# The gate of a differential attention kernel is multiplied in by GpSimd when a group leaves PSUM

## The chip, the cores and the metric

One core of one Trainium2 chip runs the kernel. The metric is the device time of one execution in microseconds, the median of several runs. Nothing below the 0.2% that separates runs of the same kernel (2296.99 to 2302.23 us here) is read as a change.

## What is computed

The reference is one layer of a transformer with differential attention: an adaptive RMS norm of 2048 latent tokens and 256 context tokens, a projection to q, k, v and a gate z, two softmaxes for each head, a norm over each head's 128 output channels, the gate, an output projection, the residual and a last RMS norm. What matters here is the end of it:

```python
def diff_attend(q, k, v, lam):
    s = jnp.einsum('bqhzd,bkhzd->bhzqk', q, k).astype(jnp.float32)
    p = jax.nn.softmax(s, axis=-1)
    a = p[:, :, 0] - lam * p[:, :, 1]
    return jnp.einsum('bhqk,bkhe->bqhe', a.astype(v.dtype), v)
...
    def finish(o, z):
        of = o.astype(jnp.float32)
        of = of * lax.rsqrt(jnp.mean(of * of, axis=-1, keepdims=True) + SUBLN_EPS)
        of = of * subln_gain.astype(jnp.float32) * (1.0 - lambda_init)
        return (of.reshape(B, L, D).astype(z.dtype) * jax.nn.silu(z)) @ w_out
```

There are 8 heads, 2048 queries and 2304 keys. The value that goes into the last matmul is thus, for each head, channel and query, the product of three numbers: the attention output `o`, a factor `f` of the query (the norm) and the gate (silu of z times the gain of the channel).

## The kernel before

The kernel works in three stages, each with a list of steps that a planner (`Plan`) puts in order from the costs and due times written beside each step. Each compute engine executes its instructions in that order. The DMA transfers are all issued from SyncE's queue (SP), in one order too, so a transfer that waits holds up those behind it.

`project` (0 to about 830 us) makes q, k, v and the gate and stores them to DRAM; the gate goes to `gate_d[h]`, one tile of 128 channels by 2048 queries for each head.

`attend` (about 830 to 2110 us) goes through 64 groups, 8 for each head, of 256 queries each (two units of 128, `u`, and two softmaxes, `z`). In a group TensorE computes the scores (`qk`, L688) into PSUM in chunks of 768 keys, VectorE copies each chunk to SBUF and keeps its minimum (`keep`, L699), ScalarE takes the exponentials (`expo`, L717), VectorE a reciprocal (`ratio`, L721), and then GpSimd weighs the second softmax (`weigh`, L729) and adds it to the first (`join`, L733). The joined probabilities are turned by TensorE (`turn`, L740), split into a high and a low part by ScalarE (`high`, L749) and VectorE (`low`, L754, which reads the low part's source from PSUM and the high part from SBUF), and multiplied with v (`pv`, L763). The turn of a group is planned some ten chunks after its scores, so TensorE has scores of the next groups to do meanwhile. At the end of a group ScalarE copies the output from PSUM to the tile `ot` (`evac`, L771), which is stored to `o_d[h]`; GpSimd clamps a copy of it (`clamp`, L776), ScalarE squares it (L779, L783), GpSimd takes the low part (`sq_low`, L787), and TensorE sums the squares (L792). After the last group of a head GpSimd computes the factor f of all its 2048 queries (`root`, nine small instructions, L823 to L831), which goes to `f_d[h]`.

`finish` (about 2090 us to the end) multiplies with the output weights. It works in four blocks of 512 queries. For each block and head, `Last.load` brings `o`, `gate` and `f` from DRAM, GpSimd multiplies o by f (`mul1`, L970), VectorE multiplies by the gate (`mul2`, L974), ScalarE and VectorE split the result (`high`, L980; `low`, L984), and TensorE multiplies (L1033). The first block of heads 0 to 6 is prepared already during the last head of `attend`; these steps are named gload, gmul1, gmul2, ghigh and glow. The three tiles of a load have two buffers, which the planner knows as the resource O.

All of L970, L974 and L984 read two tiles from SBUF; the `low` of the attention (L754) reads one from PSUM and one from SBUF.

Of the kernel before, what the change touches and what calls it, by code (L numbers as in the profile page):

```python
# [54 lines left out]
def build(tc, x, c, ctx, c_ctx, norm_gain, ada_w, ada_b, final_gain, w_in,  # L55
          lam_q, lam_k, subln_gain, w_out, cos_t, sin_t, out):
    nc = tc.nc
    with ExitStack() as top:
# [35 lines left out]

        last = Last(tc, gate_d, o_d, f_d, wo_d)
        ph = top.enter_context(ExitStack())
        with ExitStack() as inner:
            attend(tc, ph, inner, early, last, ident, ones, mhalf, sums, neglam, q_d, k_d, v_d, o_d, s_d, f_d)

# [7 lines left out]
class Plan:  # L107
# [85 lines left out]
def project(tc, ph, attend_early, ones, x, ctx, c, c_ctx, norm_gain, ada_w, ada_b, w_in, lam_q, lam_k, subln_gain,  # L193
# [296 lines left out]
    def z_gain(nm):  # L490
        nc.gpsimd.tensor_scalar(tiles["z", nm], tiles["z", nm], sgain[:, 0:1], 1.0, op0=ALU.mult, op1=ALU.mult)

# [149 lines left out]

def attend(tc, ph, inner, early, last, ident, ones, mhalf, sums, neglam, q_d, k_d, v_d, o_d, s_d, f_d):
    nc = tc.nc
# [89 lines left out]

    def turn(g, b):
        pt = ps_t.tile([P, 512], F32, tag="t", name=f"t{g}_{b}")
        for e in range(KPER):
            for u in range(G):
                kt = b * KPER + e
                nc.tensor.transpose(pt[:, (e * G + u) * P:(e * G + u + 1) * P],  # L740
                                    unit[g, u].p[0][:, kt * P:(kt + 1) * P], ident)
                yield
        group[g].t = getattr(group[g], "t", {})
        group[g].t[b] = [pt, None, None]
# [23 lines left out]
    def evac(g):  # L768
        h, i = divmod(g, NG)
        group[g].o = op.tile([P, GQ], F32, tag="ot", name=f"ot{g}")  # L770
        nc.scalar.copy(group[g].o, po2[:, g % 2])  # L771
        nc.sync.dma_start(o_d[h][:, i * GQ:(i + 1) * GQ], group[g].o)

    def clamp(g):
        group[g].sq = op.tile([P, GQ], F32, tag="sq", name=f"sqo{g}")
        nc.gpsimd.tensor_scalar(group[g].sq, group[g].o, 2.0 ** 59, -(2.0 ** 59), op0=ALU.min, op1=ALU.max)  # L776

    def square(g):
# [15 lines left out]
    def ssq_out(g):  # L794
        h, i = divmod(g, NG)
        row = op.tile([1, GQ], F32, tag="row", name=f"row{g}")
        nc.scalar.copy(row, group[g].m[0:1, :GQ])
        nc.sync.dma_start(s_d[h][i * G:(i + 1) * G].rearrange("a q -> (a q)").unsqueeze(0), row)
# [22 lines left out]
    def root(h):  # L821
        hd = head[h]
        nc.gpsimd.tensor_scalar(hd.mk, hd.r0, 2.0 ** -28, 1.0, op0=ALU.mult, op1=ALU.mult)  # L823
        nc.gpsimd.tensor_tensor(hd.u, hd.ssq, hd.mk, op=ALU.mult)
        nc.gpsimd.tensor_tensor(hd.u, hd.u, hd.mk, op=ALU.mult)
        nc.gpsimd.tensor_scalar(hd.mk, hd.u, 2.0 ** 72, 1.0, op0=ALU.is_lt, op1=ALU.mult)
# [31 lines left out]
    for g in range(TOTAL):  # L858
# [42 lines left out]
    for h in range(H - 1):  # L901
        due = ((H - 1) * NG + h) * PER
        first = [("qk", (H - 1) * NG - 1, G - 1, 1, NC - 1)] + ([("f_out", h)] if h == H - 2 else [])
        step("gload", "SP", 2300, due, last.load, (0, h), first, take=["O"])
        step("gmul1", "Pool", 1250, due + 4, last.mul1, (0, h), [("gload", 0, h)])
        step("gmul2", "DVE", 602, due + 5, last.mul2, (0, h), [("gmul1", 0, h)])
        step("ghigh", "Activation", 520, due + 6, last.high, (0, h), [("gmul2", 0, h)])
        step("glow", "DVE", 602, due + 7, last.low, (0, h), [("ghigh", 0, h)], give=["O"])
# [26 lines left out]
class Last:  # L935


    def __init__(self, tc, gate_d, o_d, f_d, wo_d):
        self.tc, self.nc = tc, tc.nc
        self.wo_d = wo_d  # L940
        self.w = {}
        self.gate_d, self.o_d, self.f_d = gate_d, o_d, f_d
        self.stack = ExitStack()
        self.pools = {}
        self.t = {}

    def open(self):
        self.io = self.stack.enter_context(self.tc.tile_pool(name="gio", bufs=2, side="right"))
        self.pools[0] = self.stack.enter_context(self.tc.tile_pool(name="g0", bufs=1, side="right"))
# [8 lines left out]
    def load(self, b, h):  # L958
        nc, sl = self.nc, slice(b * 512, (b + 1) * 512)
        o = self.io.tile([P, 512], F32, tag="o", name=f"o{b}_{h}")  # L960
        gate = self.io.tile([P, 512], F32, tag="gate", name=f"gate{b}_{h}")
        f = self.io.tile([P, 512], F32, tag="f", name=f"f{b}_{h}")
        nc.sync.dma_start(o, self.o_d[h][:, sl])
        nc.sync.dma_start(gate, self.gate_d[h][:, sl])
        nc.sync.dma_start(f, self.f_d[h][b * 4:b * 4 + 4].rearrange("a q -> (a q)").partition_broadcast(P))
        self.t[b, h] = SimpleNamespace(o=o, gate=gate, f=f)
# [20 lines left out]
def finish(tc, ph, last, x, final_gain, mhalf, gt_d, out):  # L987
# [9 lines left out]
    XB, YB = 3, 3  # L997
    plan = Plan(O=2, Y=4, X=XB, V=YB, **{f"G{p}{h}": int(p) for p in range(2) for h in range(H)})
    done = {}
# [86 lines left out]
    def heads_steps(b, h, due):  # L1086
        step("gload", "SP", 2300, due - 8, last.load, (b, h), [("f_out",)] if (b, h) == (0, H - 1) else [], take=["O"])
        step("gmul1", "Pool", 1250, due - 6, last.mul1, (b, h), [("gload", b, h)])
        step("gmul2", "DVE", 602, due - 5, last.mul2, (b, h), [("gmul1", b, h)])
        take = [f"G{b % 2}{h}"] if b else []  # L1090
        step("ghigh", "Activation", 520, due - 4, last.high, (b, h), [("gmul2", b, h)], take=take)
        step("glow", "DVE", 602, due - 4, last.low, (b, h), [("ghigh", b, h)], give=["O"])
# [91 lines left out]
```

## Time and profile before

| | us |
|---|---|
| median of 3 runs | 2298.7 (2296.99 to 2302.23) |
| the profiled execution, its own time | 2306.51 |
| span of its instructions | 2304.3 |
| TensorE busy in the span | 2234.4 (97%) |
| VectorE busy | 1621.4 (70%) |
| ScalarE busy | 1272.5 (55%) |
| GpSimd busy | 1444.9 (63%) |

The profile is one execution; sums are made against its 2306.51 us, of which 2.2 us lie outside the span of the instructions. The engines are PE (TensorE), DVE (VectorE), ACT (ScalarE), POOL (GpSimd) and SP (SyncE). In the middle of the attention a head takes 153.4 us, a group 19.2 us.

### The profile page before, as it was taken

How to read it: one execution, taken by the hardware profiler on the slowest of the kernel's cores; microseconds unless marked ns; L12 is line 12 of the kernel's file. 1: busy time of each engine (PE TensorE's matmuls, PEld its weight loads, DVE VectorE, ACT ScalarE, POOL GpSimd, SP SyncE). 2: the span in 40 equal slices, each digit the busy share in tenths (PEclk: the TensorE clock that was granted, in tenths of full speed). 3: DMA queues.
4: the chain of work that ended last, by engine and by line, in shares of the span. 5: the costliest groups of instructions: out<-in, count | busy, mean ns of one | idle time of the engine just before them, and what ended most of it. 6: DMA issues, size and time to landing. Idle time of an engine off the chain costs nothing.

```text
span 2304.3 us, 37788 instructions
## 1 busy us (share of the span) xinstructions
PE 2234.4 (97%) x14353; PEld 2061.4 (89%) x14353; DVE 1621.4 (70%) x3486; ACT 1272.5 (55%) x1909; POOL 1444.9 (63%) x747
## 2 busy tenths in 40 slices
PE   6999999999999999999999999999999997899988
PEld 5987888898888879999999999999999997898777
DVE  6755434363323359998999989999899999884663
ACT  5612322132212148887888878888788885674221
POOL 2433233353322358888888888898888987784543
PEclk9999999999999999999999999999999999999999
DMA  9865644545443251231321412313214123215772
GB/s 310 287 221 189 224 145 170 165 132 176 136 137 110 92 178 35 51 102 35 77 77 35 117 36 51 102 36 76 77 35 116 37 57 112 70 44 186 229 231 83
DMA packets 201162, 275.45 MB, mean 120 GB/s; under 512 B 13469, under 2 KB 147221, under 8 KB 195861
## 3 DMA queue, kind: packets, MB, share of 16 engines
q1 hardware_dynamic: 200980, 273.04, 38.2%
q8 instruction: 113, 1.85, 0.3%
q14 instruction: 69, 0.56, 0.1%
HBM read 184.78 MB, written 88.22 MB: 118 GB/s over the span
## 4 chain that ended last, share of the span: by engine, by line
PE 69%; DVE 11%; ACT 6%; POOL 6%; DMA 4%; issue 4%; SPq 0%; POOLq 0%; ACTq 0%; DVEq 0%
PE s L688 15%; PE po L763 12%; PE t L740 7%; PE py L1033 5%; ACT p L717 4%; DVE p L699 4%; DVE lo L754 2%; POOL p L733 1%; DMA o<-od 1%; ACT hi L749 1%; PE m21vl L446 1%; PE m23vl L446 1%; PE m22vl L446 1%; PE m13vl L446 1%; PE m12vl L446 1%
## 5 line engine op out<-in xcount | busy, mean ns | idle before, releaser
L699 DVE TENSOR_SCALAR_CACHE_REDUCE p<-s 128x768 f32<-128x768 f32 x768 | 724.4, 951 | 64.2 <-PE s L688 56.1
L688 PE MATMUL s<-k,q 128*128 128x384 f32 x3072 | 700.1, 353 | 8.9 <-DVE p L699 7.3
L733 POOL TENSOR_TENSOR p<-p,p 128x2304 f32<-128x2304 f32 x128 | 663.4, 5183 | 10.3
L717 ACT ACTIVATE p<-p,st 128x2304 f32<-128x2304 f32 x256 | 569.7, 2225 | 165.9 <-DVE st L706 165.4
L688 PEld LDWEIGHTS s<-k,q 128*128 128x128 f32 x3072 | 508.2, 191 | 19.7 <-DVE p L699 17.7
L763 PE MATMUL po<-hi,v 128*128 128x256 f32 x2304 | 504.9, 286 | 0.0
L754 DVE TENSOR_TENSOR lo<-t,hi 128x512 fp32r<-128x512 f32 x576 | 389.7, 686 | 69.4 <-ACT hi L749 63.6
L729 POOL TENSOR_SCALAR p<-p,st 128x2304 f32<-128x2304 f32 x128 | 292.5, 2285 | 167.8 <-DVE st L721 110.1
L763 PEld LDWEIGHTS po<-hi,v 128*128 128x128 f32 x2304 | 394.8, 191 | 2.3 <-ACT hi L749 0.5
L749 ACT CAST hi<-t 128x512 fp32r<-128x512 f32 x576 | 323.3, 578 | 92.1 <-PE t L740 89.2
L740 PE MATMUL t<-ident,p 128*128 128x128 f32 x2304 | 347.5, 274 | 1.3 <-POOL p L733 1.3
L763 PE MATMUL po<-lo,v 128*128 128x256 f32 x1152 | 329.3, 286 | 19.2 <-DVE lo L754 19.2
L740 PEld LDWEIGHTS t<-ident,p 128*128 128x128 f32 x2304 | 276.7, 141 | 10.5 <-POOL p L733 1.6
L763 PEld LDWEIGHTS po<-lo,v 128*128 128x128 f32 x1152 | 220.1, 191 | 23.2 <-DVE lo L754 22.5
L1033 PE MATMUL py<-wo,gh 128*128 128x512 f32 (+1 forms) x528 | 164.2, 394 | 7.1 <-ACT gh L980 6.7
L1033 PEld LDWEIGHTS py<-wo,gh 128*128 128x128 f32 x528 | 98.9, 191 | 30.2 <-ACT gh L980 7.5
L1033 PE MATMUL py<-wo,gl 128*128 128x512 f32 (+1 forms) x264 | 103.9, 394 | 1.5 <-DVE gl L984 1.5
L980 ACT CAST gh<-o 128x512 fp32r<-128x512 f32 x32 | 19.8, 620 | 97.1 <-DVE o L974 94.2
L1046 POOL TENSOR_TENSOR fv<-fv,fx 128x512 f32<-128x512 f32 x30 | 42.3, 1423 | 42.0 <-DVE fv L1041 38.8
L699 DVE DVE_READ_ACCUMULATOR p<-s 128x1 f32 x768 | 63.5, 83 | 0.0
L974 DVE TENSOR_TENSOR o<-o,gate 128x512 f32<-128x512 f32 x32 | 41.0, 1283 | 31.3 <-POOL o L970 31.3
L1033 PEld LDWEIGHTS py<-wo,gl 128*128 128x128 f32 x264 | 50.3, 190 | 14.3 <-DVE gl L984 3.2
(593 smaller groups left out, 3893.5 us busy)
## 6 DMA issues: line engine op xcount, KB each, us to landing
q<-qd SPq DMA_DIRECT2D x256, 128.0 KB
k<-kd SPq DMA_DIRECT2D x32, 576.0 KB
v<-vd SPq DMA_DIRECT2D x16, 1152.0 KB
aw<-in_ada_w SPq DMA_DIRECT2D x12, 1024.0 KB
xl<-in_x SPq DMA_DIRECT2D x16, 512.0 KB
wod<-hlwo SPq DMA_DIRECT2D x16, 512.0 KB
od<-ot SPq DMA_DIRECT2D x64, 128.0 KB
o<-od SPq DMA_DIRECT2D x32, 256.0 KB
```

Of the source, the lines that this page charges most:

```text
L446: nc.tensor.matmul(tiles["m", nm][:, t * 256:(t + 1) * 256], tok[:, j, ts], ww[:, j], start=(i == 0), stop=(i == 3 * NCH - 1))
L688: nc.tensor.matmul(ps[:, b, :CK // 2], group[g].q[:, z, f, u * P:(u + 1) * P], head[h].k[:, z, k0:k0 + CK // 2], start=(f == 0), stop=(f = ...
L699: nc.vector.tensor_scalar(un.p[z][:, ck * CK:(ck + 1) * CK].rearrange("p (b k) -> p b k", b=2), un.s[z, ck][:, :, :CK // 2], -0.125, None, ...
L717: nc.scalar.activation(un.p[z], un.p[z], AF.Exp, bias=un.st[:, 6 + z:7 + z], scale=-1.0, accum_out=acc)
L729: nc.gpsimd.tensor_scalar(p[1], p[1], st[:, 9:10], st[:, 10:11], op0=ALU.mult, op1=ALU.mult)
L733: nc.gpsimd.tensor_tensor(p[0], p[0], p[1], op=ALU.add)
L740: nc.tensor.transpose(pt[:, (e * G + u) * P:(e * G + u + 1) * P], unit[g, u].p[0][:, kt * P:(kt + 1) * P], ident)
L749: nc.scalar.copy(t[1], t[0])
L754: nc.vector.tensor_tensor(t[2], t[0], f32(t[1]), op=ALU.subtract)
L763: nc.tensor.matmul(po, head[h].v[:, vi, kt], tt[:, e * GQ:(e + 1) * GQ], start=(kt == 0 and n == 0), stop=(kt == KT - 1 and n == 2))
L1033: nc.tensor.matmul(py[r, i], aa[:, ts], w[h][:, f, sl], start=(h == 0 and n == 0), stop=(h == H - 1 and n == 2))
L1046: eng.tensor_tensor(ys[r][:, sl], ys[r][:, sl], xs[r][:, sl], op=ALU.add)
```

## The change

The gate leaves the last stage and enters the group. Two blocks of a group's matmuls before its end, `turn` issues a load of the group's 128x256 piece of the gate; when the group's values have left PSUM and are clamped, a new GpSimd step `gated` multiplies them by it in place, and only then are they stored to `o_d`. In `Last`, the gate's tile, its load and `mul2` are gone, and the pool of a load has three buffers instead of two (two tiles each instead of three, so the memory is the same). To keep the stored numbers in range the gate is scaled by 2^-35 and the factor f by 2^35, in instructions that exist already. `row`, the tile of a group's sums, has one buffer instead of two.

```diff
+F_SCALE = 2.0 ** 35
...
     def z_gain(nm):
-        nc.gpsimd.tensor_scalar(tiles["z", nm], tiles["z", nm], sgain[:, 0:1], 1.0, op0=ALU.mult, op1=ALU.mult)
+        nc.gpsimd.tensor_scalar(tiles["z", nm], tiles["z", nm], sgain[:, 0:1], 1.0 / F_SCALE, op0=ALU.mult, op1=ALU.mult)
...
     def turn(g, b):
+        if b == NB - 2:
+            h, i = divmod(g, NG)
+            group[g].gate = op.tile([P, GQ], F32, tag="gate", name=f"gate{g}", bufs=1)
+            nc.sync.dma_start(group[g].gate, gate_d[h][:, i * GQ:(i + 1) * GQ])
...
         nc.scalar.copy(group[g].o, po2[:, g % 2])
-        nc.sync.dma_start(o_d[h][:, i * GQ:(i + 1) * GQ], group[g].o)
...
+    def gated(g):
+        h, i = divmod(g, NG)
+        nc.gpsimd.tensor_tensor(group[g].o, group[g].o, group[g].gate, op=ALU.mult)
+        nc.sync.dma_start(o_d[h][:, i * GQ:(i + 1) * GQ], group[g].o)
...
-        row = op.tile([1, GQ], F32, tag="row", name=f"row{g}")
+        row = op.tile([1, GQ], F32, tag="row", name=f"row{g}", bufs=1)
...
-    plan = Plan(S=S_BUFS, T=T_BUFS, A=A_BUFS, B=2, HI=TP_BUFS, LO=TP_BUFS, O=2)
+    plan = Plan(S=S_BUFS, T=T_BUFS, A=A_BUFS, B=2, HI=TP_BUFS, LO=TP_BUFS, O=3)
...
         step("clamp", "Pool", 1029, due + 6, clamp, (g,), [("evac", g)])
+        step("gated", "Pool", 620, due + 7, gated, (g,), [("clamp", g)])
...
         step("gmul1", "Pool", 1250, due + 4, last.mul1, (0, h), [("gload", 0, h)])
-        step("gmul2", "DVE", 602, due + 5, last.mul2, (0, h), [("gmul1", 0, h)])
-        step("ghigh", "Activation", 520, due + 6, last.high, (0, h), [("gmul2", 0, h)])
+        step("ghigh", "Activation", 520, due + 6, last.high, (0, h), [("gmul1", 0, h)])
...
     def open(self):
-        self.io = self.stack.enter_context(self.tc.tile_pool(name="gio", bufs=2, side="right"))
+        self.io = self.stack.enter_context(self.tc.tile_pool(name="gio", bufs=3, side="right"))
...
-        gate = self.io.tile([P, 512], F32, tag="gate", name=f"gate{b}_{h}")
         f = self.io.tile([P, 512], F32, tag="f", name=f"f{b}_{h}")
         nc.sync.dma_start(o, self.o_d[h][:, sl])
-        nc.sync.dma_start(gate, self.gate_d[h][:, sl])
...
-    def mul2(self, b, h):
-        t = self.t[b, h]
-        self.nc.vector.tensor_tensor(t.o, t.o, t.gate, op=ALU.mult)
```

`finish` has the same edit in its own steps (gmul2 out, O=3). Three places show how the planner now orders the work.

On GpSimd, one group in the middle of the attention; `p` are the probabilities of one unit, `sqo` the clamped copy, `ot` the group's values, `sh` the squares' high and low parts. Before:

```order
L776 TENSOR_SCALAR sqo_8868<-ot_8829 128x256
L729 TENSOR_SCALAR p_8_1_8777<-p_8_1_8777,st_1_8709 128x2304
L733 TENSOR_TENSOR p_8_1_8710<-p_8_1_8710,p_8_1_8777 128x2304
L787 TENSOR_TENSOR sh_8903<-sqo_8868,sh_8903 128x256
L729 TENSOR_SCALAR p_9_0_8895<-p_9_0_8895,st_0_8837 128x2304
L733 TENSOR_TENSOR p_9_0_8838<-p_9_0_8838,p_9_0_8895 128x2304
```

and of the change, a later group at the same place:

```order
L780 TENSOR_SCALAR sqo_12482<-ot_12432 128x256
L730 TENSOR_SCALAR p_22_1_12382<-p_22_1_12382,st_1_12309 128x2304
L734 TENSOR_TENSOR p_22_1_12310<-p_22_1_12310,p_22_1_12382 128x2304
L784 TENSOR_TENSOR ot_12432<-ot_12432,gate_12346 128x256
L796 TENSOR_TENSOR sh_12511<-sqo_12482,sh_12511 128x256
L730 TENSOR_SCALAR p_23_0_12503<-p_23_0_12503,st_0_12445 128x2304
```

The new multiply (L784) stands not behind the clamp but a weigh and a join later, ahead of `sq_low` and of the next weigh.

On VectorE, the start of the last head, where the first block of head 0 is prepared; L974 is `mul2`, L984 (L987 in the change) the `low` behind it, RECIPROCAL the `ratio` that lets GpSimd start a weigh. Before:

```order
L974 TENSOR_TENSOR o_0_20734<-o_0_20734,gate_0_20735 128x512
L721 RECIPROCAL st_0_20746<-st_0_20746 128x1
L754 TENSOR_TENSOR lo_7_20935<-t_7_20906,hi_7_20922 128x512
L699 TENSOR_SCALAR p_56_1_20872,st_1_20871<-s_1_0_2_20913 128x768
L984 TENSOR_TENSOR gl_0_20943<-o_0_20734,gh_0_20942 128x512
```

and of the change:

```order
L700 TENSOR_SCALAR p_56_1_21030,st_1_21029<-s_1_0_2_21073 128x768
L722 RECIPROCAL st_0_20905<-st_0_20905 128x1
L987 TENSOR_TENSOR gl_0_21089<-o_0_20894,gh_0_21088 128x512
L759 TENSOR_TENSOR lo_7_21117<-t_7_21066,hi_7_21096 128x512
L707 TENSOR_SCALAR st_1_21029<-st_1_21029 128x3
```

One of the two VectorE steps with both inputs in SBUF is gone from each head's preparation, and the other stands here directly behind the reciprocal.

On SP's queue, the end of the attention, where the output weights (`wo`, 1 MB each) are loaded; `od` is the store of a group's values, `sd` that of its sums. Before:

```order
L956 DMA wo_22834<-wod_109 128x2048
L956 DMA wo_23181<-wod_114 128x2048
L956 DMA wo_23181<-wod_115 128x2048
L772 DMA od_99<-ot_22972 128x256
L798 DMA sd_123<-row_22997 1x256
```

and of the change:

```order
L965 DMA wo_22997<-wod_109 128x2048
L965 DMA wo_23352<-wod_114 128x2048
L740 DMA gate_23097<-gate_91 128x256
L785 DMA od_99<-ot_22995 128x256
L965 DMA wo_23352<-wod_115 128x2048
L785 DMA od_99<-ot_23137 128x256
```

The gate of the last group but one is loaded behind three of these weights, and the stores of values now stand where GpSimd has multiplied.

## Rows read from the trace of the kernel before

**Rows 1.** The page's first part: busy us (share of the span) xinstructions.

```profile
PE 2234.4 (97%) x14353; PEld 2061.4 (89%) x14353; DVE 1621.4 (70%) x3486; ACT 1272.5 (55%) x1909; POOL 1444.9 (63%) x747
```

**Rows 2.** Busy time by windows: last head first, then the head before it.

```profile
core 0: us, PE busy (x) PEld busy (x) DVE busy (x) ACT busy (x) POOL busy (x), PEclk, DMA share, GB/s
1893.40:2083.10 189.70, 167.23 (x1122) 160.91 (x1120) 171.17 (x361) 127.96 (x192) 146.82 (x67) 0.93 0.28 78
1740.00:1893.40 153.40, 153.32 (x1130) 151.04 (x1129) 139.69 (x352) 124.28 (x185) 133.61 (x58) 1.00 0.24 67
```

**Rows 3.** TensorE's waits in the last head: us in total, times, longest.

```profile
PE po L763 <- DVE lo L754: 17.9, 9, 3.6
PE s L688 <- DVE p L699: 4.6, 2, 4.3
```

**Rows 4.** The last head's window, VectorE: line 974 alone, then line 984 alone.

```profile
1893.40:2083.10 189.70, 17.99 (x8) 0.93 0.28 78
1893.40:2083.10 189.70, 17.79 (x7) 0.93 0.28 78
```

**Rows 5.** Timeline of the last head, GpSimd and VectorE: start, us, instruction [idle before].

```profile
1922.75 5.10 POOL L733 TENSOR_TENSOR p<-p,p 128x2304 f32<-128x2304 f32 x1
...
1950.15 2.28 POOL L729 TENSOR_SCALAR p<-p,st 128x2304 f32<-128x2304 f32 x1 [6.92 <-DVE st L721]
...
1923.61 4.79 DVE L984 TENSOR_TENSOR gl<-o,gh 128x512 fp32r<-128x512 f32 x1
...
1946.92 0.68 DVE L984 TENSOR_TENSOR gl<-o,gh 128x512 fp32r<-128x512 f32 x1
```

**Rows 6.** Groups of instructions, 860 to 1893.4 us: busy us, mean ns | idle before.

```profile
L733 POOL TENSOR_TENSOR p<-p,p 128x2304 f32<-128x2304 f32 x109 | 564.4, 5178 | 8.8
...
L729 POOL TENSOR_SCALAR p<-p,st 128x2304 f32<-128x2304 f32 x108 | 246.9, 2286 | 120.0 <-DVE st L721 81.6 <-PE t L740 36.7
L787 POOL TENSOR_TENSOR sh<-sqo,sh 128x256 fp32r<-128x256 f32 x53 | 39.6, 747 | 0.0
```

**Rows 7.** GpSimd's timeline, one group in the middle of the attention.

```profile
1232.61 0.75 POOL L787 TENSOR_TENSOR sh<-sqo,sh 128x256 fp32r<-128x256 f32 x1
1234.93 2.30 POOL L729 TENSOR_SCALAR p<-p,st 128x2304 f32<-128x2304 f32 x1 [1.57 <-DVE st L721]
...
1244.20 2.29 POOL L729 TENSOR_SCALAR p<-p,st 128x2304 f32<-128x2304 f32 x1 [1.23 <-DVE st L721]
```

**Rows 8.** GpSimd's root of a head, first and last instruction; windows around it and of seven heads.

```profile
1031.44 0.20 POOL L823 TENSOR_SCALAR mk<-r 128x16 f32<-128x16 f32 x1
...
1037.32 0.22 POOL L831 TENSOR_TENSOR u<-u,mk 128x16 f32<-128x16 f32 x1
...
1030.00:1060.00 30.00, 29.48 (x212) 28.27 (x211) 26.36 (x65) 23.72 (x35) 28.02 (x19) 1.00 0.15 44
...
860.00:1893.40 1033.40, 1031.53 (x7567) 1014.78 (x7566) 936.89 (x2340) 833.87 (x1239) 893.63 (x377) 1.00 0.22 63
```

**Rows 9.** TensorE's timeline in the final stage where it waited, and two windows there.

```profile
2146.50 0.74 PE L1033 MATMUL py<-wo,gh 128*128 128x512 f32 x2 [1.23 <-ACT gh L980]
...
2159.05 0.50 PE L1033 MATMUL py<-wo,gl 128*128 128x512 f32 x1 [0.77 <-DVE gl L984]
2209.21 1.22 PE L1033 MATMUL py<-wo,gh 128*128 128x512 f32 x2 [5.51 <-ACT gh L980]
...
2210.00:2220.00 10.00, 9.58 (x33) 7.33 (x32) 7.09 (x11) 1.96 (x4) 4.47 (x5) 0.73 0.67 212
2220.00:2230.00 10.00, 10.00 (x44) 8.07 (x43) 6.62 (x8) 2.59 (x6) 6.36 (x6) 1.00 0.68 203
```

**Rows 10.** Waits between 2107 and 2215 us: us in total, times, longest.

```profile
POOL o L970 <- DMA o<-od: 17.4, 7, 4.6
```

**Rows 11.** SP's queue: waits in the last head; weights issued at its end.

```profile
SPq L965 <- POOL o L970: 37.9, 7, 11.1
...
2082.66 11.66 SPq L956 DMA_DIRECT2D wo<-wod  x3
```

More of the change, by code (lines that the diff above doesn't have):

```diff
@@ L93, in build @@
                     cos_t, sin_t, ident, mhalf, sgain, neglam, gt_d, q_d, k_d, v_d, gate_d, w_out, wo_d, sums)
-        last = Last(tc, gate_d, o_d, f_d, wo_d)
+        last = Last(tc, o_d, f_d, wo_d)
         ph = top.enter_context(ExitStack())
         with ExitStack() as inner:
-            attend(tc, ph, inner, early, last, ident, ones, mhalf, sums, neglam, q_d, k_d, v_d, o_d, s_d, f_d)
+            attend(tc, ph, inner, early, last, ident, ones, mhalf, sums, neglam, q_d, k_d, v_d, gate_d, o_d, s_d, f_d)
         with ExitStack() as inner:
@@ L640, in load_q, with attend @@
     return qt
-def attend(tc, ph, inner, early, last, ident, ones, mhalf, sums, neglam, q_d, k_d, v_d, o_d, s_d, f_d):
+def attend(tc, ph, inner, early, last, ident, ones, mhalf, sums, neglam, q_d, k_d, v_d, gate_d, o_d, s_d, f_d):
     nc = tc.nc
@@ L825, in root @@
         nc.gpsimd.tensor_tensor(hd.u, hd.u, hd.mk, op=ALU.mult)
-        nc.gpsimd.tensor_scalar(hd.mk, hd.u, 2.0 ** 72, 1.0, op0=ALU.is_lt, op1=ALU.mult)
+        nc.gpsimd.tensor_scalar(hd.mk, hd.u, 2.0 ** 72, F_SCALE, op0=ALU.is_lt, op1=ALU.mult)
         nc.gpsimd.tensor_scalar(hd.u, hd.u, 2.0 ** 72, 2.0 ** 49, op0=ALU.min, op1=ALU.mult)
@@ L935, with __init__ @@
 class Last:
-    def __init__(self, tc, gate_d, o_d, f_d, wo_d):
+    def __init__(self, tc, o_d, f_d, wo_d):
         self.tc, self.nc = tc, tc.nc
@@ L941, in __init__ @@
         self.w = {}
-        self.gate_d, self.o_d, self.f_d = gate_d, o_d, f_d
+        self.o_d, self.f_d = o_d, f_d
         self.stack = ExitStack()
@@ L960, in load @@
         o = self.io.tile([P, 512], F32, tag="o", name=f"o{b}_{h}")
-        gate = self.io.tile([P, 512], F32, tag="gate", name=f"gate{b}_{h}")
         f = self.io.tile([P, 512], F32, tag="f", name=f"f{b}_{h}")
         nc.sync.dma_start(o, self.o_d[h][:, sl])
-        nc.sync.dma_start(gate, self.gate_d[h][:, sl])
         nc.sync.dma_start(f, self.f_d[h][b * 4:b * 4 + 4].rearrange("a q -> (a q)").partition_broadcast(P))
-        self.t[b, h] = SimpleNamespace(o=o, gate=gate, f=f)
+        self.t[b, h] = SimpleNamespace(o=o, f=f)
     def mul1(self, b, h):
@@ L997, in finish @@
     XB, YB = 3, 3
-    plan = Plan(O=2, Y=4, X=XB, V=YB, **{f"G{p}{h}": int(p) for p in range(2) for h in range(H)})
+    plan = Plan(O=3, Y=4, X=XB, V=YB, **{f"G{p}{h}": int(p) for p in range(2) for h in range(H)})
     done = {}
@@ L1088, in heads_steps @@
         step("gmul1", "Pool", 1250, due - 6, last.mul1, (b, h), [("gload", b, h)])
-        step("gmul2", "DVE", 602, due - 5, last.mul2, (b, h), [("gmul1", b, h)])
         take = [f"G{b % 2}{h}"] if b else []
-        step("ghigh", "Activation", 520, due - 4, last.high, (b, h), [("gmul2", b, h)], take=take)
+        step("ghigh", "Activation", 520, due - 4, last.high, (b, h), [("gmul1", b, h)], take=take)
         step("glow", "DVE", 602, due - 4, last.low, (b, h), [("ghigh", b, h)], give=["O"])
```

## The prediction

> **What bounds the kernel now.** I read the page first, then windows by head, then the waits of TensorE where the windows showed a loss, then the timelines of the engines that it waited for.
>
> TensorE is busy 97% of the span [rows 1], so an engine beside it matters only where TensorE loses time. In seven heads it loses next to nothing: 1031.5 of 1033.4 us busy [rows 8], at the full granted clock. The last head is another matter. The same work (1122 matmul records against 1130) takes 189.7 us instead of 153.4, so 36.3 us are lost there [rows 2]. Of these, 22.5 us are idle, and all of it waits for VectorE [rows 3]; the rest, about 14 us, is matmuls that ran longer: the granted clock's mean is 0.93 there, part of the time at 1.2 instead of 2.4 GHz, right after such stalls.
>
> What holds VectorE up is visible in two timelines side by side [rows 5]. A `glow` (L984) that starts at 1923.61 during a join takes 4.79 us and ends half a microsecond after the join does (1922.75 + 5.10 = 1927.85); one at 1946.92, in the 6.92 us that GpSimd is idle before 1950.15, takes 0.68. VectorE's steps with both inputs in SBUF wait out whatever GpSimd is doing. In the last head there are fifteen of them, eight `mul2` with 17.99 us and seven `glow` with 17.79 [rows 4]: 35.8 us in all, as good as the 36.3 us lost. In the heads before there are none. VectorE's order is fixed, so a `keep` or a `low` behind a blocked step waits too, and TensorE for those: it has no other work in its order.
>
> The final stage loses less. TensorE waits for a prepared head three times that count, 1.23, 0.77 and 5.51 us, and after the last it runs 33 matmuls in 10 us instead of 44, at a clock of 0.73 [rows 9], which costs another 11 x 10/44 = 2.5 us: 10.0 us together. Behind it stands the chain of load, `mul1`, `mul2`, `high`, `low` through two buffers; GpSimd waits there seven times for a load, 17.4 us [rows 10].
>
> **The change part by part.**
>
> *The last head.* Eight `mul2` leave VectorE. If every microsecond of blocked VectorE costs TensorE the same, their share is 36.3 x 17.99 / 35.8 = 18.2 us. The seven `glow` stay. They wait longest when they fall into a join, and by the order of the change some now stand directly or two steps behind the reciprocal that starts a weigh, where at most 2.3 us [rows 6] lie ahead instead of 5.2; one (head 5) still falls into the middle of a join. I take 20 us. Upper bound: the seven take 1.2 us each, 8.4 of the 36.3 stay, 28 us gain. Lower bound: half of the idle 22.5 us and none of the slow clock, 11, less 1 for a fuller GpSimd: 10 us.
>
> *The final stage.* 24 `mul2`, 24 gate loads of 256 KB and one of three issues per load go; a third buffer comes. The loads of the first heads of each block can start a buffer earlier, and the chain is a step shorter. I take 9 of the 10 us; bounds 0 (the loads are late for another reason) and 11.
>
> *GpSimd in the heads.* 64 new multiplies of 128x256 with two inputs: the nearest row is `sq_low`, same shape, 0.747 us [rows 6], 48 us in all. What hides them is idle time before a weigh: 1.57 and 1.23 us in one group [rows 7], 120 us over 53 groups [rows 6], 2.3 us per group. The new multiply leaves 1.5. Where the cover is thin is behind a root: 1031.44 to 1037.54, 6.1 us in one piece [rows 8]. GpSimd now works that off in 6.1/2.3 = 2.6 groups, later in 4. Around the root TensorE loses 0.52 of 30 us today [rows 8]. I let that double at six roots: 3 us lost. Bounds: 0, because the planner has the new step's cost and moves the turns; and 13.5, if 0.75 us of three groups shows at each of six roots.
>
> A rule speaks against this part. The Trainium skill, "GPSIMD Engine Reference", section Engine selection, sends elementwise multiplies to VectorE, since GpSimd is about two times slower with two inputs. By it the same 512 columns would go from 0.68 to some 1.4 us of engine time, a loss wherever GpSimd is short. The rows here agree on the free durations (0.68 for VectorE's two-input step [rows 5], 2 x 0.747 for GpSimd's) and differ on what was paid: 17.99/8 = 2.25 us on VectorE in the last head [rows 4]. Its case is the second rival below.
>
> *The gate's loads and the stores.* The bytes are the same (64 x 128 KB for 32 x 256 KB), spread over the heads, where the transfer engines are busy 22% [rows 8]. The load is issued two blocks of matmuls ahead, and its consumer stands a weigh and a join behind the clamp, some 8 us later [rows 6], so it is hidden. Behind a waiting `gated` on GpSimd stand `sq_low` and the next weigh, and TensorE waits for the turn. SP's queue can delay a gate: it waits up to 11.1 us for a load's buffer in the last head [rows 11], against a whole group of 19 us between free buffer and use. At the end of the attention, the gates of the last two groups stand behind weights of 1 MB, of which three took 11.66 us to issue, with waits [rows 11]. A load of this queue was waited for 4.6 us at the longest [rows 10]; I take 1 us, bounds 0 and 9 (twice 4.6). The constants, the store moved behind `gated`, and `row`'s single buffer (used once in a group) cost nothing: they add no instruction, and the store's value is read only in the last head.
>
> *Sum.* 20 + 9 - 3 - 1 = 25 us. Against the profiled execution's 2306.5 that is 2281.5; the runs shown have a median of 2298.7, 7.8 below it, and the same 25 us give **2274 us**.
>
> **The rivals.**
>
> *The blocks pass on to `glow` (chance 0.15).* With `mul2` gone, `glow` might meet joins more often. Seven times a whole join and its own time are 7 x (5.18 + 0.69) = 41 us, more than today's 35.8, and the last head gains nothing. For it speaks that joins fill over half of GpSimd's time; against it, that today's seven cost 17.8 and the new order puts several at a weigh. The Trainium skill, "SBUF — State Buffer", section SBUF: two separate sides, has the two engines share a port pair that whoever starts first holds for the whole instruction; by that rule such a `glow` is never partly hidden, and the trace agrees (4.79 us above). Time: 9 - 3 - 1 = 5 gained, 2294 us.
>
> *GpSimd becomes the bound; slower (0.06).* Today it is busy 133.6 of a head's 153.4 us; 8 x 0.75 make it 139.6, and in the last head 146.8 + 6 = 152.8 [rows 2], about all that a head at TensorE's pace has. It decides from the point where a root's 6.1 us is not worked off before the turn of that group is due. Then each of seven roots shows whole, 43 us, against 29 gained: 2298.7 + 43 - 29 = 2313 us. Against it: 1.5 us per group stay free, and the turn is planned ten chunks behind.
>
> *The final stage gains nothing (0.15).* The transfers there could be limited by their number, not by the gate. 20 - 3 - 1 = 16: 2283 us.
>
> *Everything at its lower end (0.06).* 10 gained in the last head, none at the end, 8 lost in heads: within 0.2% of 2298.7, about what a measurement of this kernel can tell from no change.
>
> **How the numbers follow.** The forecast with both gains has 0.58, and 2264 to 2284 us as its own range. With the third rival and most of the first it makes eight in ten: 2260 (28 + 11 gained, nothing lost) to 2294. Faster: 0.58 + 0.15 + 0.13 = 0.86. The rest of the first rival goes, with most of the fourth, to no change, 0.07; slower 0.07.
>
> **What would show it.** Last head: shorter than 189.7 us, near 170; no L974; VectorE's two-input steps at 10 to 18 us; TensorE's waits there under 12 us, its clock above 0.93. Heads before: 153.4 to 154 us each, the new multiply at 0.75 us without a wait for a load. Final stage: no wait of several us before the third block, GpSimd's waits for loads well under 17 us. I am wrong if heads 0 to 6 grow by a microsecond or more each (GpSimd), if the `glow`s take over 25 us (the port), or if `gated` waits for its load.

## The result, and the profile after

The changed kernel takes 2272.2 us (median of 4 runs, 2269.65 to 2275.36) against 2299.2 for the kernel before beside it (4 runs): ratio 0.9863 [0.9841, 0.9885], 27.0 us faster. A second measurement, shown below as a run of its own, gave 2272.7 against 2303.3, ratio 0.9857 [0.9819, 0.9895]. The forecast was 2274.

The profiled execution after took 2269.65 us, with a span of 2267.9; the one before had 2306.5 and 2304.3. Between these two profiles lie 36.4 us, more than between the medians, so the question is what of it belongs to the change. First the profile's row of busy time after, which answers to [rows 1] (PEld are TensorE's weight loads): TensorE is 11.5 us less busy, VectorE 38 us less, and GpSimd 48 us more.

```profile
PE 2222.9 (98%) x14353; PEld 2044.3 (90%) x14353; DVE 1583.0 (70%) x3454; ACT 1270.1 (56%) x1909; POOL 1492.9 (66%) x811
```

Then the span in three parts. A cut that is the same place in every kernel is the issue of a head's key load: from the one near 970 us to the one near 1739 lie five whole heads, from there to the start of the last score matmul the last two heads (heads 6 and 7, counted from 0), and behind that the final stage. The counts of matmuls, which agree within three, show that the parts hold the same work. Columns as in [rows 2]; first before, then after.

```profile
971.55:1738.84 767.29, 765.49 (x5609) 752.24 (x5608) 694.74 (x1735) 619.84 (x920) 665.37 (x286) 1.00 0.24 66
1738.84:2081.50 342.66, 320.11 (x2244) 311.54 (x2243) 310.44 (x710) 251.73 (x375) 279.99 (x124) 0.96 0.26 73
2081.50:2304.30 222.80, 206.86 (x978) 167.92 (x976) 116.35 (x176) 54.78 (x124) 102.40 (x89) 0.98 0.58 189
```

```profile
968.50:1739.69 771.19, 770.34 (x5612) 749.26 (x5611) 694.32 (x1736) 618.32 (x922) 691.98 (x326) 1.00 0.26 73
1739.69:2057.20 317.51, 309.47 (x2244) 299.41 (x2243) 287.66 (x703) 251.29 (x375) 291.61 (x141) 1.00 0.28 80
2057.20:2267.90 210.70, 202.62 (x978) 166.35 (x976) 100.77 (x152) 54.62 (x123) 105.93 (x91) 1.00 0.51 169
```

Five heads lose 3.9 us; the last two gain 25.15; the final stage gains 12.1; and everything ahead of 970 us (`project` and most of head 0, which holds only the first few of the new multiplies) was 3.05 shorter. That is the whole 36.4. The 3.05 are within the scatter of that part: the key load came between 966.6 and 972.8 us in thirteen of the fourteen profiles. In the last two heads TensorE has the same 2244 matmuls. Its idle time falls from 22.6 to 8.0 us and its busy time from 320.1 to 309.5, with the granted clock's mean up from 0.96 to 1.00: 14.5 us are waits that are gone, and 10.6 are shorter matmul time, which goes with less time at the 1.2 GHz level behind such waits.

The waits of TensorE over the last head after, which answer to [rows 3], and VectorE's line 987 (`glow`, formerly L984) alone, which answers to [rows 4]:

```profile
PE s L689 <- DVE p L700: 3.6, 3, 2.0
PE pss L801 <- POOL sh L796: 2.9, 2, 2.6
PE po L768 <- DVE lo L759: 1.1, 1, 1.1
PE pf L844 <- POOL u L840: 0.4, 1, 0.4
```

```profile
1894.40:2058.00 163.60, 12.63 (x7) 1.00 0.29 86
```

The longest wait is 2.6 us, and the granted clock's mean is 1.00. That longest wait is a new one: it is for GpSimd's `sq_low`, which made TensorE wait nowhere in [rows 3]. The seven `glow`s take 12.63 us instead of 17.79. The timeline of GpSimd, and of VectorE at the same places, shows two of the seven:

```profile
1927.64 2.54 POOL L977 TENSOR_TENSOR o<-o,f 128x512 f32<-128x512 f32 x2
1930.18 2.73 POOL L730 TENSOR_SCALAR p<-p,st 128x2304 f32<-128x2304 f32 x1
1932.99 5.15 POOL L734 TENSOR_TENSOR p<-p,p 128x2304 f32<-128x2304 f32 x1
...
1929.62 1.12 DVE L987 TENSOR_TENSOR gl<-o,gh 128x512 fp32r<-128x512 f32 x1
...
1935.29 3.41 DVE L987 TENSOR_TENSOR gl<-o,gh 128x512 fp32r<-128x512 f32 x1
```

One falls into a join and waits it out (1932.99 + 5.15 = 1938.14, the `glow` ends at 1938.70). The other waits 0.56 us for the end of `mul1` at 1930.18 and then runs; now it is the weigh that is held up, 2.73 us instead of 2.28 [rows 5].

In the final stage TensorE waits for no prepared head any more. These are all its waits from 2057 us on, where [rows 9] had 1.23, 0.77 and 5.51:

```profile
PE pss L801 <- POOL sh L796: 0.8, 1, 0.8
PE t L745 <- POOL p L734: 0.5, 1, 0.5
```

The new multiply takes 0.74 us at the median, and one of 64 waits for its gate. Below are GpSimd's wait, and SP's queue where that gate (L740) was late; it stands behind weights (L965), as the prediction feared for the last two groups:

```profile
POOL ot L784 <- DMA gate<-gate: 4.6, 1, 4.6
```

```profile
2057.92 11.63 SPq L965 DMA_DIRECT2D wo<-wod  x2
2069.91 0.32 SPq L740 DMA_DIRECT2D gate<-gate  x1
```

TensorE has passed its last score by then, and its waits just shown (1.3 us in all) bound what this cost.

The 3.9 us of the five heads are not idle time of TensorE (0.85 us after, 1.8 before) but weight loads that start late; meanwhile the matmuls ahead of them count as busy. Below are the weight loads of the scores (`s`) and of the sums of squares (`pss`) over these five heads, before and after; the last columns are the idle time before them and what ended it:

```profile
L688 PEld LDWEIGHTS s<-k,q 128*128 128x128 f32 x1919 | 315.4, 189 | 2.2 <-DVE p L699 1.9
...
L792 PEld LDWEIGHTS pss<-sh,ones 128*2 128x2 f32 x80 | 6.8, 85 | 2.7 <-POOL sh L787 1.4
```

```profile
L689 PEld LDWEIGHTS s<-k,q 128*128 128x128 f32 x1920 | 315.0, 189 | 7.8 <-DVE p L700 7.6
...
L801 PEld LDWEIGHTS pss<-sh,ones 128*2 128x2 f32 x80 | 6.7, 83 | 4.8 <-POOL sh L796 2.1
```

### The profile page after: what moved, and what is told of

Its sections match the earlier page's. It is cut to its first block, busy times and chain, and to the rows that moved or that the text cites. A ratio compares the mean times of both kernels' runs of the same rounds, so it can differ in the third digit from the quotient of the medians.

```text
span 2267.9 us, 37842 instructions
## 1 busy us (share of the span) xinstructions
PE 2222.9 (98%) x14353; PEld 2044.3 (90%) x14353; DVE 1583.0 (70%) x3454; ACT 1270.1 (56%) x1909; POOL 1492.9 (66%) x811
## 4 chain that ended last, share of the span: by engine, by line
PE 82%; POOL 6%; DVE 5%; DMA 3%; issue 3%; ACT 2%; SPq 0%; POOLq 0%; ACTq 0%; DVEq 0%
PE s L689 20%; PE po L768 15%; PE t L745 9%; PE py L1036 8%; POOL p L734 2%; POOL p L730 1%; DVE p L700 1%; PE m23vl L447 1%; PE m22vl L447 1%; PE m21vl L447 1%; PE m13vl L447 1%; PE m12vl L447 1%; PE m11vl L447 1%; PE m20vl L447 1%; PE m13zl L435 1%
## 5 line engine op out<-in xcount | busy, mean ns | idle before, releaser
L689 PEld LDWEIGHTS s<-k,q 128*128 128x128 f32 x3072 | 504.9, 189 | 26.6 <-DVE p L700 24.5
L1036 PEld LDWEIGHTS py<-wo,gh 128*128 128x128 f32 x528 | 98.0, 188 | 22.6 <-DMA wo<-wod 0.2
L1053 ACT ACTIVATE fx<-fv 128x512 f32<-128x512 f32 (+1 forms) x33 | 20.4, 620 | 89.4 <-POOL fv L1049 82.5
L987 DVE TENSOR_TENSOR gl<-o,gh 128x512 fp32r<-128x512 f32 x32 | 40.4, 1282 | 18.0 <-ACT gh L983 17.6
```

The lines of the kernel that those rows point to most:

```text
L689: nc.tensor.matmul(ps[:, b, :CK // 2], group[g].q[:, z, f, u * P:(u + 1) * P], head[h].k[:, z, k0:k0 + CK // 2], start=(f == 0), stop=(f = ...
L1036: nc.tensor.matmul(py[r, i], aa[:, ts], w[h][:, f, sl], start=(h == 0 and n == 0), stop=(h == H - 1 and n == 2))
```

## The experiments

The theory at this point: the last head's gain is VectorE no longer held up by GpSimd (and TensorE's clock, which follows), the final stage's is a late preparation that is no longer late, and the multiply on GpSimd is nearly free. Twelve runs were made. The table gives what each profile showed: the five heads, the last two heads and TensorE's idle time in them, the two-input steps of VectorE's preparation there (`mul2` and `glow`: sum, count), and the final stage. All in us. The planner orders all steps anew for every edit, so no run changes a step alone; the five heads, which take 767.3 to 767.8 us wherever GpSimd has no new multiply, show how little that moves where nothing else changes.

| kernel | median | five heads | last two heads | idle there | steps | final stage |
|---|---|---|---|---|---|---|
| before | 2299.2 | 767.3 | 342.7 | 22.6 | 35.8 (15) | 222.8 |
| before_again | 2301.2 | 767.4 | 339.9 | 21.9 | 34.9 (15) | 223.6 |
| third_buffer | 2297.1 | 767.6 | 345.2 | 26.6 | 39.1 (15) | 211.3 |
| final_stage_only | 2293.4 | 767.4 | 338.1 | 22.5 | 30.5 (14) | 210.6 |
| no_mul2_last_head | 2283.6 | 767.4 | 325.7 | 12.2 | 15.1 (8) | 221.9 |
| mul2_on_gpsimd | 2274.1 | 767.3 | 312.8 | 5.2 | 9.6 (8) | 223.4 |
| no_gated | 2271.1 | 767.4 | 319.0 | 9.6 | 13.9 (7) | 210.9 |
| after | 2272.2 | 771.2 | 317.5 | 8.0 | 12.6 (7) | 210.7 |
| after_again | 2272.7 | 771.3 | 318.8 | 6.5 | 11.9 (7) | 210.6 |
| two_buffers | 2269.2 | 771.1 | 316.6 | 5.8 | 11.9 (7) | 210.7 |
| gate_from_psum | 2264.5 | 767.8 | 313.6 | 5.6 | 10.0 (7) | 210.7 |
| low_on_scalar | 2264.8 | 771.2 | 313.0 | 3.8 | 0 | 210.7 |
| both_moved | 2262.7 | 767.7 | 312.0 | 4.4 | 0 | 211.0 |
| gated_thrice | 2299.9 | 786.0 | 322.3 | 9.9 | 8.9 (7) | 215.2 |

**no_mul2_last_head**: the kernel before, with only the last head's seven multiplies left out.

```diff
-        step("gmul2", "DVE", 602, due + 5, last.mul2, (0, h), [("gmul1", 0, h)])
-        step("ghigh", "Activation", 520, due + 6, last.high, (0, h), [("gmul2", 0, h)])
+        step("ghigh", "Activation", 520, due + 6, last.high, (0, h), [("gmul1", 0, h)])
```

> The kernel before, with mul2 left out for the seven heads of block 0 that are prepared in the last head (the gate is still loaded but not multiplied into them; the final stage is as before). If blocked VectorE steps are what the last head loses, it falls from 188 us to 162 to 168 us and the final stage stays near 222 us: a median of 2274 to 2280 us. If the loads or the number of buffers are what counts, nothing of that is touched and the time stays above 2292 us.

Measured: 2283.55 us, ratio 0.9928 [0.9902, 0.9954]; the last two heads fall to 325.7, the final stage stays at 221.9. The gain is in the last head, as said, but the time is above what the theory gave, and 325.7 is 8 more than the changed kernel, with `glow`s nearly as cheap (14.45 us for seven). Most of the rest sits at one place. VectorE's timeline has the one multiply that still falls into this head (head 7's, prepared early for the final stage), and TensorE's the wait that followed; the windows behind it show the clock:

```profile
1988.16 0.69 DVE L973 TENSOR_TENSOR o<-o,gate 128x512 f32<-128x512 f32 x1 [4.86 <-POOL o L969]
...
1989.59 0.58 PE L763 MATMUL po<-lo,v 128*128 128x256 f32 x1 [4.21 <-DVE lo L754]
```

```profile
1980.00:1990.00 10.00, 5.79 (x43) 5.56 (x42) 5.14 (x13) 3.45 (x6) 7.98 (x4) 0.94 0.15 43
1990.00:2000.00 10.00, 9.77 (x52) 9.10 (x51) 7.60 (x16) 7.83 (x14) 7.28 (x3) 0.72 0.13 39
2000.00:2010.00 10.00, 7.95 (x47) 7.92 (x48) 8.59 (x19) 5.44 (x8) 5.08 (x5) 0.83 0.32 91
```

So a multiply on VectorE has a second price that the prediction did not name: it stands at the head of VectorE's fixed order and waits for GpSimd's `mul1`, here 4.86 us, with every `keep` and `low` behind it.

**final_stage_only**: the complement; the multiply is left out in the steps of `finish` alone. One of these, head 7's, falls into the last head, so 14 steps stay there and not 15.

```diff
-        step("gmul2", "DVE", 602, due - 5, last.mul2, (b, h), [("gmul1", b, h)])
...
-        step("ghigh", "Activation", 520, due - 4, last.high, (b, h), [("gmul2", b, h)], take=take)
+        step("ghigh", "Activation", 520, due - 4, last.high, (b, h), [("gmul1", b, h)], take=take)
```

> The kernel before, with VectorE's multiply by the gate left out in the final stage alone (head 7 of block 0 and all heads of blocks 1 to 3 go ungated); the last head keeps its seven multiplies, and everything has two buffers as before. Theory (the two gains are separate: the last head's stalls and the final stage's late sixth and seventh heads): from the last score to the end of the span 210.5 to 212 us instead of 222.8 to 223.6, nothing else changed, so 2287 to 2292 us and a ratio near 0.995. Rival (the final stage is shorter only because the attention ahead of it is, or because of the third buffer): 222 us there still, and 2297 to 2302 us.

Measured: 2293.44 us (10 runs), ratio 0.9956 [0.9936, 0.9976], 1.4 above the upper end that I gave. Its final stage is as expected, while the last two heads take 338.1 us, a little under the 339.9 and 342.7 of the two profiles of before:

```profile
2075.10:2285.70 210.60, 202.94 (x978) 166.51 (x977) 93.96 (x152) 55.34 (x125) 103.95 (x89) 0.99 0.51 172
```

The two gains are separate: 210.6 here, 221.9 in the run above. With one step gone the steps of the last head are 5.3 us shorter, yet TensorE's idle time is as before (22.5). In its place stands one wait for GpSimd's `sq_low`, which neither profile of before has at that length:

```profile
PE pss L792 <- POOL sh L787: 6.7, 1, 6.7
```

**third_buffer**: the kernel before with three buffers instead of two for the prepared heads, in the pool and in the plans of the attention and the final stage. To make room, six small tiles of the attention got one buffer instead of two.

```diff
-        self.io = self.stack.enter_context(self.tc.tile_pool(name="gio", bufs=2, side="right"))
+        self.io = self.stack.enter_context(self.tc.tile_pool(name="gio", bufs=3, side="right"))
...
-    plan = Plan(O=2, Y=4, X=XB, V=YB, **{f"G{p}{h}": int(p) for p in range(2) for h in range(H)})
+    plan = Plan(O=3, Y=4, X=XB, V=YB, **{f"G{p}{h}": int(p) for p in range(2) for h in range(H)})
```

> The kernel before with three buffers for a load (five small tiles of a group or head get one buffer instead of two, to make room) and everything else as before. My theory: all fifteen blocked VectorE steps are still there, so the last head stays at 183 to 193 us; the final stage may gain up to 8 us: 2291 to 2299 us. If the buffer is what counts, 2280 us or less.

Measured: 2297.09 us (10 runs), ratio 0.9975 [0.9954, 0.9997]. Its window of the final stage:

```profile
2084.30:2295.60 211.30, 203.13 (x978) 166.51 (x976) 119.94 (x176) 54.98 (x125) 103.82 (x88) 0.99 0.58 194
```

**two_buffers**: the changed kernel with two buffers, the same three places put back.

```diff
-    plan = Plan(S=S_BUFS, T=T_BUFS, A=A_BUFS, B=2, HI=TP_BUFS, LO=TP_BUFS, O=3)
+    plan = Plan(S=S_BUFS, T=T_BUFS, A=A_BUFS, B=2, HI=TP_BUFS, LO=TP_BUFS, O=2)
```

> The changed kernel with two buffers for a load instead of three. By my theory the last head keeps its gain (162 to 168 us), since no VectorE step comes back, and the final stage gives back a part of its 12 us, because the chain of a load still has to go through two buffers: 2273 to 2282 us. If the third buffer makes the gain, the time goes back to 2290 us or more.

Measured: 2269.18 us, ratio 0.9865 [0.9831, 0.9898], below the span that I gave; the final stage takes 210.7 us and gives nothing back. Either part alone, the buffer or the shorter chain, brings the final stage to some 211 us, and the second one adds nothing. In third_buffer only about half of that gain reaches the time (the ratio is worth 5.8 us); its last two heads, 345.2 in the one profile, are the longest of all. Whether that comes from the third buffer or from the tiles made single is not shown. GpSimd's waits for loads in the final stage, 17.4 us before [rows 10], are as long in two_buffers, and TensorE waits there for no prepared head:

```profile
POOL o L977 <- DMA o<-od: 20.7, 7, 8.2
```

**no_gated**: the changed kernel without its new multiply and without the gate's loads.

```diff
-        step("gated", "Pool", 620, due + 7, gated, (g,), [("clamp", g)])
```

> The changed kernel without the new multiplies and the gate's loads (the gate is left out altogether; values are stored right behind the evacuation). It prices the 64 multiplies. My theory: the heads before the last gain 1 us in all, the last head 0 to 4 us, the rest nothing: 2267 to 2272 us. If GpSimd, busy 94% of the last head in the changed kernel, is what bounds that head now, it falls from 163 to 157 us or less, and the time to 2266 us or less.

Measured: 2271.13 us, ratio 0.9877 [0.9838, 0.9917], 1.1 below the changed kernel, less than either scatters. The profiles are sharper: the five heads take 767.44 us without the multiply and 771.1 to 771.3 in four profiles with it. The multiply on GpSimd thus costs about 0.77 us a head. I had given 1 us in all for the heads before the last.

**gated_thrice**: two_buffers with each multiply made three times, twice into a tile that nobody reads.

```diff
+        for _ in range(2):
+            dup = op.tile([P, GQ], F32, tag="dup", name=f"dup{g}", bufs=1)
+            nc.gpsimd.tensor_tensor(dup, group[g].o, group[g].gate, op=ALU.mult)
         nc.gpsimd.tensor_tensor(group[g].o, group[g].o, group[g].gate, op=ALU.mult)
...
-        step("gated", "Pool", 620, due + 7, gated, (g,), [("clamp", g)])
+        step("gated", "Pool", 1860, due + 7, gated, (g,), [("clamp", g)])
```

> The changed kernel with two buffers (2269.2 us), where GpSimd multiplies each group's values by the gate three times, twice into a tile that nobody reads: 1.5 us more of GpSimd for each of 64 groups, 12 us a head. Theory (GpSimd has 15.4 us of room in a head before the last and 11 in the last one): the heads before the last stay within 3 us in all, the last head gets 2 to 12 us longer, 2270 to 2284 us. Rival (GpSimd's order is what counts, and any work put between its joins delays them): each head 5 to 12 us longer, 2310 us or more. If GpSimd had room to spare everywhere: 2267 to 2271 us.

Measured: 2299.91 us (10 runs), ratio 0.9999 [0.9975, 1.0023]: the whole gain is gone. My expectation for the heads before the last fails: they lose 14.9 us in five (786.0 against 771.1), where I gave 3 for all. The last two heads take 322.3 instead of 316.6, the final stage 215.2 instead of 210.7. Below are the window of the five heads, and TensorE's waits over the attention:

```profile
972.55:1758.57 786.02, 773.10 (x5612) 748.56 (x5611) 691.27 (x1736) 622.01 (x920) 750.37 (x406) 1.00 0.26 71
```

```profile
PE pss L804 <- POOL sh L799: 17.2, 36, 1.3
PE s L689 <- DVE p L700: 3.2, 6, 1.6
```

GpSimd is busy 750.37 of 786.02 us, so it still has 7 us free in a head, but not where it counts: `sq_low` stands behind the multiplies in its order, and TensorE reaches that group's sum of squares first. The rival's 5 to 12 us a head is not reached either; it is 3.0.

**mul2_on_gpsimd**: the kernel before, nothing left out; the last head's seven multiplies are made by GpSimd, 512 wide, with the same due time.

```diff
-        step("gmul2", "DVE", 602, due + 5, last.mul2, (0, h), [("gmul1", 0, h)])
+        step("gmul2", "Pool", 1250, due + 5, last.mul2_gpsimd, (0, h), [("gmul1", 0, h)])
```

> The kernel before, with the last head's seven multiplies by the gate on GpSimd instead of VectorE, 512 wide and in the same place; nothing is left out, and the final stage keeps VectorE's multiplies. Theory (the price in the last head was VectorE blocked by GpSimd, 2.2 us a piece, and not the work): attention as short as with the multiplies left out (1199.7 us from 860 to the last score, where the kernel before has 1215 to 1222), plus 0 to 5 us for the 9 us of GpSimd that come on top, final stage 222 to 224: 2282 to 2291 us. Rival (GpSimd has no room for them there, 145 of 188 us before, and would have 154 of some 172): its joins come late and the time is 2295 us or more.

Measured: 2274.06 us, ratio 0.9878 [0.9848, 0.9908], below the expected span. This one line brings nearly what the whole change does, although GpSimd is now busy 153.7 of 158.3 us of that head. The last two heads, then line 988 (`glow`) alone in the last one:

```profile
1733.89:2046.70 312.81, 307.59 (x2243) 300.17 (x2242) 284.67 (x703) 251.31 (x376) 288.53 (x131) 1.00 0.28 80
```

```profile
1888.41:2060.00 171.59, 8.50 (x7) 1.00 0.34 100
```

It beats no_mul2_last_head, which does less work, by 12.9 us in the last two heads: no VectorE step waits for `mul1` in this profile, and the `glow`s take 8.5 us instead of 14.45. That these two make the whole difference is argued from the profiles, not tested by itself.

**low_on_scalar**: the changed kernel, with the last head's seven `glow`s replaced by plain copies on ScalarE (the subtraction is left out).

```diff
-        step("glow", "DVE", 602, due + 7, last.low, (0, h), [("ghigh", 0, h)], give=["O"])
+        step("glow", "Activation", 520, due + 7, last.low_copy, (0, h), [("ghigh", 0, h)], give=["O"])
```

> The changed kernel with the seven low steps of the last head as copies on ScalarE (the subtraction is left out there, so the low part is a copy of the whole). It takes the last seven VectorE steps with two inputs in SBUF out of the last head. If these are what the head still loses, it falls from 163 us to 154 to 158 us: 2264 to 2269 us. If GpSimd bounds the head, it stays within 2 us of 163 and the time at 2270 to 2274 us.

Measured: 2264.77 us, ratio 0.9835 [0.9806, 0.9865]. The last two heads lose another 4.5 us (317.5 to 313.0) for 12.6 us of `glow`, 0.36 for each microsecond, where the first 23.2 us (35.8 to 12.6) brought 25. The medians (2272.2 and 2264.8) would give 0.6, so the price is lower here, but its size is not well known.

**gate_from_psum**: the changed kernel, nothing left out; VectorE multiplies the gate onto a group's values while it reads them from PSUM, and GpSimd's multiply goes. ScalarE's copy then feeds only the clamp, and the gate is loaded two blocks earlier.

```diff
-        nc.gpsimd.tensor_tensor(group[g].o, group[g].o, group[g].gate, op=ALU.mult)
+        group[g].o = op.tile([P, GQ], F32, tag="ot", name=f"ot{g}")
+        nc.vector.tensor_tensor(group[g].o, po2[:, g % 2], group[g].gate, op=ALU.mult)
...
-        step("gated", "Pool", 620, due + 7, gated, (g,), [("clamp", g)])
+        step("gated", "DVE", 340, due + 2, gated, (g,), [("pv", g, NB - 1)])
```

> The changed kernel with the gate multiplied in by VectorE, which reads the group's values from PSUM and the gate from SBUF, instead of by GpSimd; ScalarE's evacuation now feeds only the clamp. VectorE gets 64 steps of about 0.35 us, none of which GpSimd can block since only one input lies in SBUF; GpSimd loses 48 us. By my theory the last head falls by 2 to 5 us and the other heads stay within 1 us: 2266 to 2271 us. If VectorE's extra work lands on TensorE's path (VectorE is busy 91% of a head), each group pays up to 0.35 us, 20 us in all, and the time is 2275 to 2292 us.

Measured: 2264.46 us, ratio 0.9831 [0.9803, 0.9859], about 8 us below the changed kernel and under the span that I gave. The profile says where: the five heads are back at 767.8, the last two take 313.6 instead of 317.5. The multiply's own row (min/median/max in ns, over the whole attention):

```profile
L784 DVE TENSOR_TENSOR ot<-po,gate x64: 410/420/425, 874.8 to 2077.6; 128x256 f32<-128x256 f32 x64
```

Sixty-four of them, among joins that fill over half of GpSimd's time, and none was held up.

**both_moved**: gate_from_psum, with the last head's `glow`s on GpSimd besides.

```diff
-        step("glow", "DVE", 602, due + 7, last.low, (0, h), [("ghigh", 0, h)], give=["O"])
+        step("glow", "Pool", 1250, due + 7, last.low_gpsimd, (0, h), [("ghigh", 0, h)], give=["O"])
```

> The version with the gate multiplied by VectorE out of PSUM, and besides the last head's seven subtractions (glow) on GpSimd instead of VectorE; nothing is left out. Theory (what is left of the stalls in the last head is VectorE blocked in glow, about 9 to 12 us there, worth about half of that): attention 3 to 6 us shorter than the 1191.8 us of that version, 2258 to 2263 us. Rival (GpSimd, at 145.7 of 159 us in the last head there, takes 9 us more and becomes the bound): 2264 us or more, with TensorE waiting for joins (t<-p).

Measured: 2262.7 us (2258.18 to 2265.96), ratio 0.9825 [0.9795, 0.9854]. It is the lowest median, but the interval overlaps that of gate_from_psum, and the two aren't told apart. Last two heads 312.0 instead of 313.6: the expected 3 to 6 us are not there.

**before_again and after_again**: both kernels once more, to see how far profiles of one kernel differ.

> The kernel before once more, for a second profile of it. The profile shown of before is the slowest of its runs by 4 us. If its last head was unusually long, this one has 178 to 186 us there instead of 188; if not, the same 188 us, and the 9 us that the two profiles differ by beyond the medians lie in the final stage.

> The changed kernel once more, timed beside the experiments on the same chip, and a second profile of it. Expected: 2269 to 2276 us, a last head of 161 to 166 us and 209 to 212 us behind it.

Measured: 2301.22 us for one run of before, with 339.9 us in the last two heads instead of 342.7; 2272.73 for after (2265.85 to 2282.82), ratio 0.9857 [0.9819, 0.9895]. The profiled execution of after was the longest, 2282.8, though its last parts are like the first's (table). Of its extra 13.1 us, 11.8 lie ahead of the key load. The largest loss found there is at the start of the attention: a wait of TensorE for a load of queries, and a slow clock in the window around it.

```profile
PE s L689 <- DMA q<-qd: 3.9, 1, 3.9
```

```profile
860.00:880.00 20.00, 16.12 (x97) 15.58 (x96) 12.80 (x32) 9.72 (x12) 12.41 (x3) 0.83 0.17 48
```

The key load near 970 us comes at 980.3 in this execution, and at 966.6 to 972.8 in the other thirteen profiles. Parts behind it can be compared to some tenths of a microsecond in the five heads and to about 3 in the last two; whole executions cannot.

## Why the prediction was right, term by term

**The last head, +20: the mechanism held; 25 measured.** The size was 5 short. Blocked steps fell from 35.8 to 12.6 us, and the price of one to one that the prediction took nearly held for these 23 us (25.15 gained in the last two heads, which also hold one head's 0.77 of loss). Two things were mis-sized. The `glow`s got cheaper by 5.2 us, where I had allowed some 2 in all. And `mul2` also made VectorE wait for `mul1`, as no_mul2_last_head showed; in the profile of before it did so for 3.0 us. That stands in the idle column of its group in the last head, which the sum left out:

```profile
L974 DVE TENSOR_TENSOR o<-o,gate 128x512 f32<-128x512 f32 x8 | 18.0, 2249 | 3.0 <-POOL o L970 3.0
```

18.0 + 5.2 + 3.0 = 26.2, against 25.15 + 0.8 measured. In the second pair of profiles the same sum is 18.1 + 5.0 + 3.0 = 26.1 against 21.2 + 0.8, so the close agreement of the first is luck, and the price lies between 0.8 and 1. The upper bound, 28, assumed that the same price holds to the end; low_on_scalar shows that it drops, to 0.36 by the profiles.

**The final stage, +9: 12.1 measured, above the upper bound of 11.** Of the two reasons given, either suffices (third_buffer, final_stage_only), so they don't add. The sign that I named, GpSimd's waits for loads, was the wrong one: in two_buffers they last 20.7 us and cost nothing. What the waits of [rows 9] show to count is whether a head's `high` and `low` came before TensorE needed them. The waits were sized right (7.5 us in [rows 9]; TensorE's idle time in the stage falls by 7.9), the slow clock behind them too low: 2.5 us from one window, where TensorE's busy time falls by 4.2.

**Heads before the last, -3: five measured heads lose 3.9, seven at that rate 5.4; inside the bounds of 0 to 13.5.** A head takes 154.2 us, just over the 153.4 to 154 that I named as a sign. I had put the loss at the roots. The rows put it at late weight loads: the idle time before the score's grows by 5.6 us, waiting for VectorE's `keep`, and that before the sum of squares' by 2.1, in part for GpSimd's `sq_low`, the place where gated_thrice then loses most. Whether GpSimd or the planner's new order makes `keep` late is open. That no_gated and gate_from_psum are back at 767.4 and 767.8 shows only that the multiply on GpSimd brings the loss.

**Gate loads and the end, -1: at most 1.3.** The wait behind the weights came, 4.65 us long on GpSimd, with at most 1.3 us of it on TensorE.

Terms measured: 25.15 + 12.1 - 3.9 = 33.4 in the first pair of profiles, 21.2 + 13.0 - 3.9 = 30.3 in the second pair, 27.0 and 30.6 between the medians. The forecast's 25 is a little low by all of them. That 2274 came within 2 us of 2272.2 owes something to chance: a gain some microseconds too small was taken from 2298.7, and the medians of before in later runs were 2299.2 to 2303.5.

**The rivals.** The blocks did not pass on to `glow` (12.6 us, not 41). The final stage did gain. GpSimd did not become the bound at 0.75 us a group, but gated_thrice shows how near that was: 1.5 us more a group takes the whole gain back, at another place than I had named, the sum of squares and not the root.

## What to carry to other kernels

Price a step on the engine that is held up by what it waits for, not by its own duration: here 0.68 us of VectorE's work took 2.25 with the blocking, and cost more in the waits of a fixed order and the clock behind it. The Trainium skill, "GPSIMD Engine Reference", section Engine selection, would put such a multiply on VectorE. The runs here differ from it for a step that competes with long GpSimd instructions: mul2_on_gpsimd is the faster (ratio 0.9878). Before moving it to GpSimd, look whether one input is still in PSUM: gate_from_psum keeps it on VectorE and is 8 us faster than the change. In this head the first 23 us of held steps gave back nearly one for one, and the last 12.6 us less.

## What was not expected of the hardware

A VectorE multiply with one input in PSUM and one in SBUF (128x256) took 0.41 to 0.425 us in 64 of 64 cases in gate_from_psum; a subtraction with both in SBUF (128x512) took 0.67 to 3.50 us in the same run. The Trainium skill, "SBUF — State Buffer", section SBUF: two separate sides, limits the lock against GpSimd to VectorE's steps with two SBUF inputs and its two-port modes; the trace agrees on the inputs, and no run here tests the modes. The hold-up also works the other way: GpSimd's weigh took 2.73 us behind a `glow` instead of 2.28.

Stalls cost TensorE more than their length: behind one of 4.21 us the granted clock's mean was 0.72 over the next 10 us, in a window of 20 us around one of 3.9 (after_again) it was 0.83, and in the last head after the change, with waits of 2.6 at most, it stayed at 1.00.

One combination was not run: mul2_on_gpsimd with a third buffer for the final stage, 2274.1 less the 12 us between final stages of 223.4 and 211.3, an estimate of 2262 us, level with both_moved. In third_buffer only about half of such a gain reached the time, which would make it 2268.
